# The opening of a streaming encoder layer: table load, row transfers, squares and rooms for modulation slabs rearranged

## The chip, the core and the metric

The kernel runs on one core of a Trainium2 chip. A core has a matrix engine (TensorE, PE in the profile), a vector engine (VectorE, DVE), a scalar engine (ScalarE, ACT), a general engine (GpSimd, POOL) and a synchronising engine (SyncE, SP). Each works off its own list of instructions in order. Transfers between memory and the core are issued here by SP and by ACT, as instructions in those lists. The metric is the device time of one execution in microseconds; the time before is the median of three runs.

## The reference

One layer of a hybrid encoder over 2048 prompt frames and 64 sample frames, 1024 channels each. A condition vector per stream gives six modulation vectors; the first two shift and scale the normalised input of the projection:

```python
mod = jax.nn.silu(c) @ p['w_ada'] + p['b_ada']
sh1, sc1, gt1, sh2, sc2, gt2 = [m[:, None, :] for m in jnp.split(mod, 6, axis=-1)]
h = rms_norm(x, p['norm1_g']) * (1 + sc1) + sh1
z = h @ p['w_in']
glu_a, glu_b, q, k, v, g_conv, g_attn = jnp.split(z, offs, axis=-1)
u = glu_a * jax.nn.sigmoid(glu_b)
conv_out, conv_state = conv_module(u, conv_hist, ...)      # depthwise width 31, layer norm, swish, projection
o = attend(rms_norm(q), rms_norm(k), v, p['rel_bias'])     # own chunk of 64 frames and the 8 before it
merged = sigmoid(g_conv) * conv_out + sigmoid(g_attn) * (o @ p['w_attn_out'])
x = x + gt1 * (merged @ p['w_o'])
# then a second modulated norm and a SwiGLU feed-forward of width 2816, with gt2
```

Everything is float32. The outputs are the two streams' rows, the last convolution rows, and the key and value rows.

## The kernel before

**Stages.** The 2112 rows are cut into four blocks (576, then three of 512). Each block goes through the projections q, k, v, the gated convolution inputs and the gates, while attention and convolution of earlier work run beside them. Then the merge, the output projection and the feed-forward run over three larger blocks of columns. Products of float32 are made of three matmuls each: weights and activations are split into a high part (ACT copies to the reduced format: `whi`, `hh`) and a low part (DVE or POOL subtracts: `wlo`, `hl`).

**The first block.** The change lies in what happens before and during the first projection, the function `first_block` and what it calls:

- `load_vectors` loads the two condition vectors (`r0`, two small transfers on ACT's queue), and later six small vectors (norm gains, convolution biases, `b_ada`) into `r1`, on SP's queue. `setup` turns `r0` into a column `cc` on PE, takes its tanh on ACT (the first function that needs ACT's table) and makes `cl` from it. Its inner function `vectors` turns `r1` into columns, `cols`.
- `Slabs` brings the modulation weights `w_ada` in slabs of 512 KB (`wmod`), into four rooms. For the first two vectors there are sixteen slabs; `modulation(ct)` uses four at a time, ct = 0, 2, 4, 6, and its part `rest` writes the columns `B1` and `A1` for two of the eight channel tiles. A slab's room is given back when PE has used it, and `fill` then issues the next load. The first four are shared between the queues of SP and ACT.
- `first_rows` loads the five row tiles of the block (64 rows, then four of 128), three on SP's queue and two on ACT's. `scale_rows` takes a row tile's sum of squares (`square`: two halves on ACT, one DVE addition, then a DVE operation and a power on POOL in `rsqrt_mean`) and scales the rows on DVE.
- `turn(k)` transposes channel tile k of all five row tiles on PE, applies `A1` and `B1` on DVE (`h32`), and splits into `hh` and `hl`. `product(i, k)` multiplies by the q weights, which `Weights` brings as `wst` tiles (512 KB each, at first one staging room, three after `W.open("wst")`) and splits.

**What sets the order.** Each engine's list is laid out when the kernel is built: an instruction's place follows the order in which the code makes it, as far as its inputs and its tile's room allow, by an estimate of times. `tc.issue_after(ins)` keeps instructions of the block, on the engine of `ins`, behind `ins`. Tiles with the same tag share a number of rooms (`bufs`); a tile that finds none waits for a release. Transfers of SP and ACT are counted on a small set of counters that go round in the order of issue. A host-side planner (`Stream`) keeps an estimated load per engine and spreads later work over PE's time; the tag `vv` (two rooms, first used by the relative bias rows `rv`, later by attention's v) and the tag `y` (one room, the convolution's output) belong to stages after the first projection.

Of the kernel before, what the change touches and what calls it, by code (L numbers as in the profile page):

```python
# [8 lines left out]
F32 = mybir.dt.float32  # L9
F32R = mybir.dt.float32r  # L10
AF = mybir.ActivationFunctionType
ALU = mybir.AluOpType
# [4 lines left out]
P = 128  # L17
D = 1024
KT = 8
# [210 lines left out]
class Slabs:  # L230
# [3 lines left out]
    def __init__(self, sync, other, pool, stream, keys, source, held):  # L234
        self.sync, self.other, self.pool, self.stream = sync, other, pool, stream
        self.keys, self.source, self.held = keys, source, held
        self.ready, self.used, self.given, self.freed = [], 0, 0, 0

    def fill(self):
        while len(self.ready) < min(len(self.keys), self.freed + self.held):  # L240
            (src,), a, b = self.source(self.keys[len(self.ready)])
            w = self.pool.tile([P, a, b], F32, tag="wmod", name="wmod", bufs=self.held)
            i = len(self.ready)
            (self.other if i < self.held and i % 2 else self.sync).dma_start(w, src)
            self.ready.append(w)

    def get(self, key):
        assert self.keys[self.used] == key
# [363 lines left out]
def streaming_layer(ctx: ExitStack, tc: tile.TileContext, I, O):  # L612
# [155 lines left out]
    def load_vectors():  # L768

        r0 = temp("r0", (16, P))  # L770
        r1 = temp("r1", (76, P))
        by_row = lambda a: a.rearrange("(r c) -> r c", c=P)
        nc.scalar.dma_start(r0[0:8], by_row(I["c_prompt"][0]))
        nc.scalar.dma_start(r0[8:16], by_row(I["c_sample"][0]))
        yield r0, r1
        o = 0
        for name in ("norm1_g", "norm2_g", "b_dw", "conv_ln_g", "conv_ln_b", "b_ada"):
            a = by_row(I[name][0])
            nc.sync.dma_start(r1[o : o + a.shape[0]], a)
            o += a.shape[0]  # L780
        yield

    def setup():
# [109 lines left out]

    def first_rows():
        places = ((wa, "x", 3), (wa, "x", 3), (wa, "x", 3), (wk, "kk", 1), (wk, "q2", 1))
        queues = (nc.sync, nc.sync, nc.scalar, nc.sync, nc.scalar)
        return [load_x(*tl, *place, q) for tl, place, q in zip(token_tiles(*PBLOCKS[0]), places, queues)]

    def first_block(xs):

# [1 line left out]
        vectors, taps, begun = setup()  # L902
        taps = taps()

        def scale_rows(a, b):
            for x_t, (t, n) in list(zip(xs, tiles))[a:b]:
                r = square(x_t, n)
                dve.tensor_scalar(x_t[:n], x_t[:n], r, None, ALU.mult)

        def modulation(ct):  # L910

# [27 lines left out]
        with tc.issue_after(begun[0]), tc.issue_after(begun[1]):  # L939
            scale_rows(0, 2)  # L940
            rest = modulation(0)
            vectors()
            rest()
            sums_turned = pe.last.ins
            with tc.issue_after(dve.last.ins):
                scale_rows(2, 5)
            with tc.issue_after(act.last.ins), tc.issue_after(dve.last.ins):
                W.reach = W.held
                W.fill()
        with tc.issue_after(sums_turned):  # L950
            turn(0)
        pss = [ps_g.tile([P, 512], F32, tag="gp", name="ps") for _ in tiles]
# [11 lines left out]
        for k in range(KT - 2):  # L964
            if k == 2:
                with tc.issue_after(act.last.ins):
                    next(taps)
            turn(k + 1)
            if k and k % 2 == 0:
                rest = modulation(k + 2)  # L970
            for i in range(len(tiles)):
                if i == 2 and not k:
                    rest = modulation(k + 2)
                    W.open("wst")
                if i == (2 if k else 4) and k % 2 == 0:
                    rest()
                product(i, k)
# [136 lines left out]
    def load_x(t, n, pool, tag, bufs, queue=nc.sync):  # L1114
        x_t = pool.tile([P, D], F32, tag=tag, name="x_t", bufs=bufs)
        queue.dma_start(x_t[:n], rows(x_p, x_s, t, n))
        return x_t

    def square(x_t, n):
# [1111 lines left out]
```

## Time and profile before

| | us |
|---|---|
| median of three runs | 3007.48 (3004.33 to 3010.57) |
| profiled execution | 3013.09 |
| its span, first to last instruction | 3011.3 |
| PE busy | 2927.7 |
| DVE busy | 2080.1 |
| ACT busy | 1291.3 |
| POOL busy | 1136.0 |

Rows of the timeline read: start, length, engine, line, operation, what it writes and from what, how many; in brackets the engine's idle time before it and what ended it. `ACTq` and `SPq` are the engines' own lists, where transfers are issued. All metered operations have line 102, that of the helper, so one goes by the names of tiles. Rows for a stretch read: stretch, length, then busy time and instructions of PE, weight loads, DVE, ACT and POOL, the granted PE clock, the share of the transfer engines, and GB/s. The chain of waits lists start, length and what the path stood on.

### The profile page before, as it was taken

How to read it: one execution, taken by the hardware profiler on the slowest of the kernel's cores; microseconds unless marked ns; L12 is line 12 of the kernel's file. 1: busy time of each engine (PE TensorE's matmuls, PEld its weight loads, DVE VectorE, ACT ScalarE, POOL GpSimd, SP SyncE). 2: the span in 40 equal slices, each digit the busy share in tenths (PEclk: the TensorE clock that was granted, in tenths of full speed). 3: DMA queues.
4: the chain of work that ended last, by engine and by line, in shares of the span. 5: the costliest groups of instructions: out<-in, count | busy, mean ns of one | idle time of the engine just before them, and what ended most of it. 6: DMA issues, size and time to landing. Idle time of an engine off the chain costs nothing.

```text
span 3011.3 us, 45036 instructions
## 1 busy us (share of the span) xinstructions
PE 2927.7 (97%) x16259; PEld 2599.9 (86%) x16259; DVE 2080.1 (69%) x3836; ACT 1291.3 (43%) x2333; POOL 1136.0 (38%) x734
## 2 busy tenths in 40 slices
PE   7999989999999999989999999999999999999999
PEld 4889767788888788888989899999999999999998
DVE  5888777877877886477776755666666556466666
ACT  3334532452254257464444435534444345344443
POOL 0201310101011102354566533256666841466667
PEclk9999899999999999999999999999999999999999
DMA  8888788888997788885444686423323875323333
GB/s 296 284 294 289 247 300 282 263 266 273 301 289 236 253 267 271 258 291 167 142 150 146 210 288 210 148 93 113 120 92 122 292 253 184 97 94 112 120 99 129
DMA packets 467725, 628.07 MB, mean 209 GB/s; under 512 B 36276, under 2 KB 314664, under 8 KB 467501
## 3 DMA queue, kind: packets, MB, share of 16 engines
q1 hardware_dynamic: 453456, 605.58, 61.6%
q10 hardware_dynamic: 14045, 19.60, 1.9%
q8 instruction: 128, 2.10, 0.3%
q14 instruction: 96, 0.79, 0.1%
HBM read 476.53 MB, written 148.54 MB: 208 GB/s over the span
## 4 chain that ended last, share of the span: by engine, by line
PE 79%; DVE 9%; DMA 6%; ACT 2%; issue 2%; POOL 2%; SPq 0%; ACTq 0%; POOLq 0%; DVEq 0%
PE ps L102 49%; PE pd L102 15%; PE pw L102 6%; DVE y L102 3%; PE po L102 2%; PE sc L102 2%; PE ptp L102 2%; DVE wlo L102 1%; PE pa L102 1%; PE pt L102 1%; DVE pr L102 1%; DMA wst<-in_w_in 1%; ACT whi L102 1%; POOL r L102 1%; POOL wlo L102 1%
## 5 line engine op out<-in xcount | busy, mean ns | idle before, releaser
L102 PE MATMUL ps<-t,whi 128*128 128x384 f32 (+1 forms) x2112 | 502.8, 322 | 9.6 <-ACT t L102 4.6
L102 POOL TENSOR_TENSOR wlo<-wst,whi 128x1024 fp32r<-128x1024 f32 (+1 forms) x157 | 357.9, 2290 | 272.2 <-ACT whi L102 258.2
L102 ACT ACTIVATE whi<-wst 128x1024 fp32r<-128x1024 f32 (+1 forms) x264 | 257.5, 978 | 331.8 <-PE ps L102 105.0
L102 PE MATMUL ps<-b,whi 128*128 128x384 f32 (+1 forms) x1584 | 381.7, 326 | 6.0 <-DVE early L102 3.4
L102 PEld LDWEIGHTS ps<-t,whi 128*128 128x128 f32 x2112 | 367.7, 188 | 16.9 <-ACT t L102 4.8
L102 DVE SCALAR_TENSOR_TENSOR y<-u,wd,y 128x512 f32<-128x512 f32 (+1 forms) x480 | 370.2, 773 | 5.8
L102 PE MATMUL ps<-hh,whi 128*128 128x512 f32 (+2 forms) x992 | 363.7, 367 | 0.0
L102 DVE TENSOR_TENSOR acc<-acc,pd 128x512 f32<-128x512 f32 (+1 forms) x464 | 311.6, 685 | 66.8 <-PE pd L102 64.4
L102 PE MATMUL ps<-hh,wlo 128*128 128x512 f32 (+2 forms) x992 | 347.7, 350 | 0.0
L102 PE MATMUL ps<-hl,whi 128*128 128x512 f32 (+2 forms) x992 | 347.0, 350 | 0.0
L102 PE MATMUL ps<-t,wlo 128*128 128x384 f32 (+1 forms) x1056 | 339.3, 321 | 0.7 <-POOL wlo L102 0.7
L102 PE MATMUL pd<-whi,hid 128*128 128x512 f32 (+1 forms) x1016 | 325.5, 391 | 0.2 <-DVE acc L102 0.2
L102 PEld LDWEIGHTS ps<-b,whi 128*128 128x128 f32 x1584 | 278.8, 190 | 12.1 <-DVE early L102 4.2
L102 PE MATMUL ps<-b,wlo 128*128 128x384 f32 (+1 forms) x792 | 257.0, 325 | 0.0
L102 POOL TENSOR_TENSOR r<-t,mhalf 128x1 f32<-128x1 f32 (+3 forms) x68 | 81.7, 1203 | 456.5 <-DVE t L102 449.6
L102 PEld LDWEIGHTS pd<-whi,hid 128*128 128x128 f32 (+1 forms) x1016 | 185.9, 183 | 45.5 <-DVE acc L102 1.1
L102 PEld LDWEIGHTS ps<-hh,wlo 128*128 128x128 f32 x992 | 188.2, 190 | 22.2
L102 PEld LDWEIGHTS ps<-hh,whi 128*128 128x128 f32 x992 | 188.7, 190 | 18.2 <-issue 2.5
L102 PEld LDWEIGHTS ps<-hl,whi 128*128 128x128 f32 x992 | 189.0, 191 | 15.6 <-issue 1.7
L102 PEld LDWEIGHTS ps<-t,wlo 128*128 128x128 f32 x1056 | 198.2, 188 | 2.2 <-POOL wlo L102 1.3
L102 PE MATMUL pd<-wlo,hid 128*128 128x512 f32 (+1 forms) x508 | 198.5, 391 | 0.0
L102 DVE TENSOR_TENSOR wlo<-wst,whi 128x1024 fp32r<-128x1024 f32 (+1 forms) x107 | 133.7, 1255 | 82.1 <-ACT whi L102 80.6
(225 smaller groups left out, 6255.1 us busy)
## 6 DMA issues: line engine op xcount, KB each, us to landing
whi<-w_din_h SPq DMA_DIRECT2D x72, 512.0 KB, 7.0
wlo<-w_din_l SPq DMA_DIRECT2D x72, 512.0 KB, 7.3
wst<-sum_d SPq DMA_DIRECT2D x132, 256.0 KB, 2.8
wfo<-in_w_ffn_out SPq DMA_DIRECT2D x64, 512.0 KB, 3.4
wmod<-in_w_ada SPq DMA_DIRECT2D x46, 512.0 KB, 7.5
sum_d<-ws SPq DMA_DIRECT2D x88, 256.0 KB, 3.1
wst<-in_w_ffn_in SPq DMA_DIRECT2D x84, 256.0 KB, 3.1
wst<-in_w_in SPq DMA_DIRECT2D x40, 512.0 KB, 8.0
```

The lines of the kernel that those rows point to most:

```text
L102: self.last = f(*args, **kw)
```

## The change

Five edits, all for the first block:

- The six small vectors of `r1` are loaded on ACT's queue, behind the tanh, instead of on SP's queue ahead of the rows. `vectors` now runs after the first sums of the modulation.
- All five row tiles are loaded on SP's queue.
- The square of a first-block row is one ACT operation over 1024 elements, written to a part of `hl` that isn't used yet, with no addition behind it. The fifth row is scaled on ACT, after the first weight's split, instead of on DVE; the third row's scaling is placed ahead of `rest`.
- Slabs 4 to 7 go to four lent rooms (two of tag `vv`, two halves of the convolution's `y`), so that they can be loaded before the first four rooms are free, and slabs 8 to 11 follow into the first four rooms.
- The staging rooms for weights are opened at once; the first split alone is made early, and the others where the rooms were opened before.

```diff
@@ class Slabs
+    def room(self):
+        i = len(self.ready)
+        if self.lent is None:
+            return i < self.held
+        n = len(self.lent)
+        return i < self.freed + self.held + (n if i < self.held + n + self.held else 0)

     def fill(self):
-        while len(self.ready) < min(len(self.keys), self.freed + self.held):
+        while len(self.ready) < len(self.keys) and self.room():
             (src,), a, b = self.source(self.keys[len(self.ready)])
-            w = self.pool.tile([P, a, b], F32, tag="wmod", name="wmod", bufs=self.held)
             i = len(self.ready)
+            if i >= self.held and i - self.held < len(self.lent):
+                w = self.lent[i - self.held]().rearrange("p (a b) -> p a b", a=a)
+            else:
+                w = self.pool.tile([P, a, b], F32, tag="wmod", name="wmod", bufs=self.held)
...
+    def lend(self, rooms):
+        self.lent = rooms
+        self.fill()
@@ load_vectors
-            nc.sync.dma_start(r1[o : o + a.shape[0]], a)
+            nc.scalar.dma_start(r1[o : o + a.shape[0]], a)
@@ setup
         act_th = act.last.ins
+        with tc.issue_after(act_th):
+            next(vectors_)
@@ first_rows
-        queues = (nc.sync, nc.sync, nc.scalar, nc.sync, nc.scalar)
-        return [load_x(*tl, *place, q) for tl, place, q in zip(token_tiles(*PBLOCKS[0]), places, queues)]
+        return [load_x(*tl, *place) for tl, place in zip(token_tiles(*PBLOCKS[0]), places)]
+
+    def lent_rooms():
+        conv_room = wk.tile([P, 4, YW], F32, tag="y", name="ym").rearrange("p c w -> p (c w)")
+        v_room = lambda: wk.tile([P, D], F32, tag="vv", name="vm", bufs=2)
+        return [v_room, v_room, lambda: conv_room[:, :D], lambda: conv_room[:, D : 2 * D]]
@@ first_block
+        def square_row(i):
+            return square(xs[i], tiles[i][1], hl[:, KT - 2 :, :512])
...
             rest = modulation(0)
-            vectors()
-            rest()
+            with tc.issue_after(pe.last.ins), tc.issue_after(dve.last.ins):
+                vectors()
+                scale_rows(2, 3)
+            with tc.issue_after(dve.last.ins):
+                rest()
             sums_turned = pe.last.ins
             with tc.issue_after(dve.last.ins):
-                scale_rows(2, 5)
+                scale_rows(3, 4)
+                r = square_row(4)
             with tc.issue_after(act.last.ins), tc.issue_after(dve.last.ins):
-                W.reach = W.held
+                W.reach = 1
                 W.fill()
+            with tc.issue_after(act.last.ins):
+                act.activation(xs[4], xs[4], AF.Copy, scale=r)
...
                     rest = modulation(k + 2)
-                    W.open("wst")
+                    W.reach = W.held
+                    W.fill()
@@ square
+        if room is not None:
+            act.activation(room[:n], x_t[:n].rearrange("p (a b) -> p a b", a=2), AF.Square, accum_out=ssq[:n, 0:1])
+            stream.after("dve", "act")
+            return rsqrt_mean(wk, ssq[:n, 0:1], n, 1, D)
@@ main
     M.fill()
-    next(vectors_)
     xs = first_rows()
     W = Weights(...)
+    M.lend(lent_rooms())
+    W.open("wst")
     first_block(xs)
```

More of the change, by code (lines that the diff above doesn't have):

```diff
@@ L237, in __init__ @@
         self.ready, self.used, self.given, self.freed = [], 0, 0, 0
+        self.lent = None
+    def room(self):
[4 more added lines that the diff above has]
+        return i < self.freed + self.held + (n if i < self.held + n + self.held else 0)
     def fill(self):
-        while len(self.ready) < min(len(self.keys), self.freed + self.held):
+        while len(self.ready) < len(self.keys) and self.room():
             (src,), a, b = self.source(self.keys[len(self.ready)])
-            w = self.pool.tile([P, a, b], F32, tag="wmod", name="wmod", bufs=self.held)
             i = len(self.ready)
+            if i >= self.held and i - self.held < len(self.lent):
+                w = self.lent[i - self.held]().rearrange("p (a b) -> p a b", a=a)
+            else:
+                w = self.pool.tile([P, a, b], F32, tag="wmod", name="wmod", bufs=self.held)
             (self.other if i < self.held and i % 2 else self.sync).dma_start(w, src)
             self.ready.append(w)
+    def lend(self, rooms):
+        self.lent = rooms
+        self.fill()
     def get(self, key):
@@ L903, in first_block @@
         taps = taps()
+        def square_row(i):
+            return square(xs[i], tiles[i][1], hl[:, KT - 2 :, :512])
         def scale_rows(a, b):
-            for x_t, (t, n) in list(zip(xs, tiles))[a:b]:
-                r = square(x_t, n)
-                dve.tensor_scalar(x_t[:n], x_t[:n], r, None, ALU.mult)
+            for i in range(a, b):
+                n, r = tiles[i][1], square_row(i)
+                dve.tensor_scalar(xs[i][:n], xs[i][:n], r, None, ALU.mult)
         def modulation(ct):
@@ L1117, in load_x, with square @@
         return x_t
-    def square(x_t, n):
+    def square(x_t, n, room=None):
         ssq = wk.tile([P, 2], F32, tag="ssq", name="ssq", bufs=3)
+        if room is not None:
+            act.activation(room[:n], x_t[:n].rearrange("p (a b) -> p a b", a=2), AF.Square, accum_out=ssq[:n, 0:1])
+            stream.after("dve", "act")
+            return rsqrt_mean(wk, ssq[:n, 0:1], n, 1, D)
         for j in range(2):
```

## The prediction

> **What bounds the kernel now.** I read the page first, then stretches of equal length, then the chain of waits at the start. The page says that TensorE (PE) is the bound over the whole run; the stretches say where it is not.
>
> ```profile
> span 3011.3 us, 45036 instructions
> PE 2927.7 (97%) x16259; PEld 2599.9 (86%) x16259; DVE 2080.1 (69%) x3836; ACT 1291.3 (43%) x2333; POOL 1136.0 (38%) x734
> ```
>
> ```profile
> 0.00:50.00 50.00, 29.32 (x186) 18.58 (x187) 22.99 (x66) 15.31 (x32) 4.27 (x14) 1.00 0.86 270
> 50.00:100.00 50.00, 48.86 (x302) 38.20 (x301) 34.39 (x63) 18.13 (x29) 9.14 (x9) 1.00 0.88 305
> 400.00:450.00 50.00, 41.95 (x185) 30.51 (x183) 35.19 (x82) 14.93 (x36) 6.97 (x6) 0.88 0.90 291
> ```
>
> PE idles 83.6 us in all (3011.3 less 2927.7), and 20.7 us of that lies in the first 50. The change touches the start alone, so it can win some of these 20.7 us and no more. The start as it runs now, by the chain of waits and then the timeline:
>
> ```profile
> 0.73 2.66 DMA r<-in_c_prompt
> 3.41 7.56 DMA x_t<-in_x_prompt
> 10.99 0.35 ACTq L1116
> 11.37 1.28 ACT L102
> 13.35 3.69 PE pa L102 x32
> ```
>
> ```profile
> 1.70 0.97 ACTq L244 DMA_DIRECT2D wmod<-in_w_ada  x2
> 1.78 0.80 SPq L779 DMA_DIRECT2D r<-in_norm_g  x2
> 4.91 0.25 SPq L779 DMA_DIRECT2D r<-in_b_dw  x1
> 5.55 0.17 DVE L102 COPY cc<-pt 128x16 f32<-128x16 f32 x1 [3.60 <-PE pt L102]
> 8.31 0.32 SPq L779 DMA_DIRECT2D r<-in_b_ada  x1
> 9.51 0.30 ACTq L989 DMA_DIRECT2D rv<-in_rel_bias  x1
> 11.67 0.36 PE L102 MATMUL pt<-ident,r 76*128 76x76 f32 x1 [6.15 <-DMA r<-in_b_ada]
> 12.66 0.21 ACT L102 ACTIVATE th<-cc 128x16 f32<-128x16 f32 x1
> 12.79 0.61 ACT L102 ACTIVATE junk<-x_t 64x512 f32<-64x512 f32 x1
> 18.21 0.63 ACT L102 ACTIVATE junk<-x_t 128x512 f32<-128x512 f32 x1 [2.80 <-issue]
> 21.29 0.61 ACT L102 ACTIVATE junk<-x_t 128x512 f32<-128x512 f32 x1
> 21.90 1.04 ACT L102 ACTIVATE whi<-wst 128x1024 fp32r<-128x1024 f32 x1
> 24.61 0.75 DVE L102 TENSOR_SCALAR x_t<-x_t,r 128x1024 f32<-128x1024 f32 x1 [0.66 <-POOL r L102]
> 28.84 0.78 PE L102 MATMUL ps<-whi,hh 128*64 128x512 f32 x1
> ```
>
> To be seen: the column `cc` is ready at 5.72, but its tanh runs at 12.66. ACT was standing in its own queue: the row tile issued at 3.41 landed at 10.97, and only then (10.99) did the next issue go, and the table load at 11.37. So an issue can wait for the landing of an earlier transfer that has nothing to do with it. SP shows the same: after 2.58 its next tiny load goes at 4.91. The first product stands at 28.84, 3.48 us after the fifth row tile was scaled (24.61 + 0.75 = 25.36).
>
> **The change part by part.** *Rows on SP, table loaded early.* ACT is free of transfers at 2.67 (1.70 + 0.97). The table load of 1.28 then ends at about 4, and tanh follows `cc` at 5.75: 6.9 us earlier. The sums of the first four slabs (3.69 us) then wait for the slabs. Four slabs are 2.10 MB, the five row tiles 2.36 MB, the first weight 0.52 MB.
>
> ```profile
> 2.00:17.00 15.00, 4.26 (x34) 1.75 (x34) 2.06 (x11) 4.03 (x10) 1.07 (x4) 1.00 1.00 332
> 60.00:70.00 10.00, 10.00 (x52) 7.62 (x51) 3.94 (x12) 1.75 (x2) 0.00 (x0) 1.00 1.03 402
> 26.00:34.00 8.00, 6.19 (x44) 3.73 (x45) 6.76 (x13) 4.30 (x6) 0.00 (x0) 1.00 0.28 76
> 90.00:110.00 20.00, 20.00 (x97) 15.46 (x96) 18.03 (x24) 4.30 (x7) 0.21 (x1) 1.00 1.02 340
> ```
>
> At 332 GB/s from 2.0 us the four slabs are there by 8.3, the rows by 9.1, 10.7, 12.3, 13.8 and 15.4, the first weight by 17.0, the four lent slabs by 23.3. The sums so end near 10, not at 17.04. They are no longer what is late; the rows are. The Trainium skill (DMA: Bandwidth & Descriptors, Specifications) puts the HBM share of a core at about 358 GB/s; by that, as an estimate, the fifth row would land 0.9 us earlier, at 14.5. The trace doesn't bear it out as a limit (402 GB/s from 60 to 70); the sum goes by the measured 332.
>
> *Six small loads moved from SP to ACT, behind tanh, ahead of the squares.* This is the unknown of the change. Each takes 0.25 to 0.40 us of issue (rows at 1.78 to 8.31), and each may wait for the landing of an earlier transfer, as ACT did at 10.99. Lower bound: no wait, six issues end at 5.95 + 6 x 0.3 = 7.8, and the squares wait only for rows. Upper bound: all of SP's new queue was issued before them, and the last of the six waits for the fourth lent slab, 23.3. I take 12.5: between the issue of the slabs and that of the six, SP has some four or five row tiles out, so the last waits are for row tiles, of which the third lands at 12.3. The vectors are then at PE 3.36 us after the last issue (11.67 less 8.31), by 15.9. What follows them:
>
> ```profile
> 19.57 1.22 PE L102 MATMUL pa<-sel,R 128*128 128x128 f32 x4 [0.54 <-DVE B L102]
> 20.83 0.16 DVE L102 TENSOR_TENSOR A<-pa,cols 128x4 f32<-128x4 f32 x1 [1.32 <-PE pa L102]
> ```
>
> Some six small DVE operations at 0.16 to 0.23 take them to 17.0; the edit puts the third row's scaling (0.75) ahead of the rest, 17.8; one more of 0.16, the second four matmuls (1.22) and two of 0.16 end at 19.5. The rows are later, as the next two steps show.
>
> *Squares in one operation.* Two halves start 0.61 to 0.63 apart. One operation over 1024 I price by the weight split of that size, 1.04, and 0.02 between: 1.06 for 1.24, and the DVE addition (0.15) behind it goes. Five rows from 12.5 end at 17.8. Rows four and five have landed (13.8, 15.4). No gap of 2.80 stands between second and third any more.
>
> *Fifth row scaled on ACT.* After the square come the weight split (1.05; the weight is there at 17.0) and the scaling, priced like the split, 1.05: done at 19.9. POOL's power for that row fits under the split. Hence the first product follows the start of the squares by 5.3 + 2.1 + 3.4 = 10.8: 12.5 + 10.8 = 23.3. **Term 1: 28.84 to 23.3, -5.5** (bounds: squares limited by the fifth row alone, first product 22.5, -6.3; upper bound 23.3 + 10.8 = 34.1, +5.3).
>
> *Second slabs in lent rooms, weights opened early.* The transfer engines are busy 0.28 of the time from 26 to 34 now: 5.8 us lost while slabs wait for rooms. With four more rooms, slabs and two weights go on without the gap. What PE waits for later in this pass:
>
> ```profile
> 47.59 0.71 PE L102 MATMUL pa<-sel,R 128*128 128x128 f32 x4 [1.70 <-DVE R L102]
> 57.06 0.64 PE L102 MATMUL pa<-wmod,cl 128*32 128x256 f32 x8 [0.41 <-DMA wmod<-in_w_ada]
> 58.43 0.64 PE L102 MATMUL pa<-wmod,cl 128*32 128x256 f32 x8 [0.73 <-DMA wmod<-in_w_ada]
> ```
>
> ```profile
> 35.69 8.91 DMA wst<-in_w_in
> ```
>
> ```profile
> ACT whi L102 <- DMA wmod<-in_w_ada: 3.8, 1, 3.8
> ```
>
> The wait of 1.70 stands behind a weight that landed at 44.60; by bytes it now lands by 36 (11.3 MB up to it at 332 GB/s). **Term 2: -1.7.** The 0.41 and 0.73 are for the last slabs, which still come one for one; I leave them (bound: -1.1 more). *The load of the bias table* (`rv`, 9.51 now) loses its early room to a slab and is issued on ACT in the middle of the pass, where ACT already stood 3.8 us behind an issue that waited for a slab. Bounds 0 and +3.8; I take 0, since PE did not stop at that wait (its only waits there are the three above).
>
> *What is kept.* -5.5 and -1.7 make -7.2 at the end of the pass. From 90 to 110 the transfers are full (1.02), so what is bound by bytes there can move up only by the idle 5.8 us filled. I take the middle of 5.8 and 7.2: **-6.5**. The later gaps move with the rest. The profiled execution took 3013.09 us, 5.6 above the median of the three runs, 3007.48; it would give 3006.6, and the median 3001.0.
>
> **The rivals.** *ACT stands behind its own small loads* (ends slower). For: the rows at 3.41 and 10.99 show the mechanism, and the six loads now stand ahead of all squares on the same engine. Against: tanh comes early, when SP can have issued little. With the squares starting at s, the first product is at s + 10.8; s = 19.7 eats both terms. At the upper bound, 34.1, it is +5.3 - 1.7 = +3.6, and with the bias load's 3.8 hitting the products +7.4: 3014.9. It passes +6 when s is over 21.9 and ACT stands 3.8 us again in the pass. In its mild form (s of 15 to 20) the time is 3004 to 3008.
>
> *The gain is swallowed.* The stretch at 90 to 110 is full of transfers and 0.90 of DVE; if DVE's work there doesn't move up, the PE gap behind it grows by what was won: 3007.5. Against: DVE's input is PE's output, which comes earlier.
>
> *A later gap opens.* In 400 to 450 PE lost 8.05 us (50 less 41.95) at a granted clock of 0.88; a shifted order could bring one more such gap: -6.5 + 8.05, 3009.0. Nothing in the rows says that it must. The Trainium skill (TensorE: Matmul & The Clock Gate, HAM oscillation) says that PE gaps beyond about 3.4 us bring the half clock back; the 0.88 of that row agrees with the rule, and it would make such a gap dearer than its idle time.
>
> *All bounds at their good end*: -6.3 - 1.7 - 1.1 = -9.1: 2998.4.
>
> **How the numbers follow.** Forecast 0.53 (-9 to -3: 2998.5 to 3004.5); small loads, mild 0.10, hard 0.15; swallowed 0.09; later gap 0.08; all good 0.05. About 0.2%, 6.0 us, is what a measurement here can tell from none. The forecast lies on that edge: 0.33 of its chance beyond it, 0.20 within. Faster 0.33 + 0.05 = 0.38; within 0.20 + 0.10 + 0.09 + 0.08 = 0.47; slower 0.15. The range, 2997.5 to 3013.5, takes in the good end and all but the worst of the small loads; the forecast's own is 2998.5 to 3004.5.
>
> **What would show it.** Tanh before 7; the first sums at PE ending near 10; squares starting near 12.5, as one operation of about 1.06 each; the fifth row scaled on ACT near 20; the first product at 22 to 25; no stretch of idle transfers between 26 and 34; no wait of 1.7 for R; the end of the pass 6 to 8 us before 75. Wrong it would be if the squares start after 16, if ACT's small loads show issue times spread over ten microseconds, or if the pass ends early and the stretch from 100 on doesn't.

## The result, and the profile after

The changed kernel takes 3014.45 us (median of 17 runs, 3007.10 to 3015.63), the kernel before, run beside it, 3010.13 us (17 runs, 3001.97 to 3014.52). The ratio is 1.0015, with a 95% interval of 1.0008 to 1.0022: slower by about 4.5 us, where 6.5 us less was forecast, and outside the range given. The two profiled executions (3013.09 before, 3012.72 after) lie at different places of their kernels' spreads, so their spans don't show the difference. The stages of the start do. Everything below is read from those.

The head of the page after:

```profile
span 3010.9 us, 45020 instructions
```

The timeline of the start after (start, length, engine, line, operation, tiles, count, and in brackets the idle time before it with what ended it):

```profile
2.37 9.56 SPq L1149 DMA_DIRECT2D x_t<-in_x_prompt  x4
2.69 1.28 ACT L102 ACT_TABLE_LOAD   x1 [2.69 <-issue]
5.28 0.21 ACT L102 ACTIVATE th<-cc 128x16 f32<-128x16 f32 x1 [1.30 <-DVE cc L102]
5.28 1.09 ACTq L795 DMA_DIRECT2D r<-in_norm_g  x2
5.97 1.08 PE L102 MATMUL pa<-wmod,cl 128*32 128x256 f32 x8 [0.94 <-DVE cl L102]
11.63 1.93 PE L102 MATMUL pa<-wmod,cl 128*32 128x256 f32 x16 [4.58 <-DMA wmod<-in_w_ada]
15.41 0.25 ACTq L795 DMA_DIRECT2D r<-in_b_dw  x1
15.43 1.08 PE L102 MATMUL pa<-wmod,cl 128*32 128x256 f32 x8 [1.87 <-DMA wmod<-in_w_ada]
16.46 0.32 ACTq L795 DMA_DIRECT2D r<-in_b_ada  x1
16.83 1.06 ACT L102 ACTIVATE hl<-x_t 64x1024 fp32r<-64x1024 f32 x1 [11.34 <-DMA r<-in_conv_ln_b]
...
21.55 1.06 ACT L102 ACTIVATE hl<-x_t 128x1024 fp32r<-128x1024 f32 x1
...
25.20 0.16 DVE L102 TENSOR_TENSOR A<-A,cols 128x4 f32<-128x4 f32 x1
25.28 0.15 DVE L102 TENSOR_SCALAR t<-ssq 128x1 f32<-128x1 f32 x1
26.77 0.15 DVE L102 TENSOR_SCALAR t<-ssq 128x1 f32<-128x1 f32 x1
26.83 1.21 DVE L102 TENSOR_TENSOR wlo<-wst,whi 128x1024 fp32r<-128x1024 f32 x1
26.99 1.46 POOL L102 TENSOR_TENSOR r<-t,mhalf 128x1 f32<-128x1 f32 x1 [0.93 <-DVE t L102]
28.49 1.15 ACT L102 ACTIVATE x_t<-x_t,r 128x1024 f32<-128x1024 f32 x1 [4.83 <-POOL r L102]
32.63 0.77 PE L102 MATMUL ps<-whi,hh 128*64 128x512 f32 x1
```

To be seen, from the top:

- The table load is early and tanh runs at 5.28 instead of 12.66. The first eight sums start at 5.97 (before: 13.35).
- But PE then stops for a slab until 11.63, and for the last slab until 15.43. The sums end at 16.51, where they ended at 17.04 before. Nearly the whole early start is lost to slabs that come late.
- ACT issues the first two of its six small loads at 5.28 and the third at 15.41. That is 0.02 us before PE picks up the last slab: the issue waited for that slab's landing, just as PE did (the same pair stands in the run with the fourth and fifth row ahead of the columns: 14.88 and 14.90). Its other loads follow in a row, and the squares start at 16.83 (before: 12.79).
- The squares themselves are one operation of 1.06, and all five are through at 22.61. The fifth row is scaled on ACT, but only at 28.49: ACT waited 4.83 us for the row's factor `r`. The DVE operation that feeds it (`t`, at 26.77) stands behind the modulation columns (`A`, 25.20) and the fourth row in DVE's list.
- The first product is at 32.63, 3.79 us later than before (28.84).

Why the slabs come late is told by the packets of the two queues (q1 is SP's, q10 ACT's: packets, MB, share of the 16 transfer engines). From 9 to 11 us after:

```profile
q1 hardware_dynamic: 152, 0.56, 77.1%
q10 hardware_dynamic: 154, 0.15, 23.3%
```

and from 7 to 9 us before:

```profile
q10 hardware_dynamic: 531, 0.74, 109.2%
q1 hardware_dynamic: 8, 0.00, 0.5%
```

After, the two queues have the same number of packets in that stretch, 152 and 154. But a packet of the rows is 3.7 KB (0.56 MB by 152), one of the slabs 1.0 KB. So SP's rows take 79% of the bytes, and the two slabs on ACT's queue get 75 GB/s. From 7 to 13 us together it is 409 and 424 packets, 1.48 and 0.42 MB. Before, SP had no row out until 8.68 (one row stood on ACT's own queue, behind its slabs), and between 7 and 9 us ACT's queue moved 0.74 MB, 370 GB/s, alone. The Trainium skill (DMA: Bandwidth & Descriptors, Queues, rings and completion order) says that a transfer engine goes round the queues that have work and takes a packet from each before it goes on. The trace agrees from 7 to 13 us: packets are shared evenly, and bytes by the size of the packets.

The later part of the pass. The end of the first pass is read at the first transposition of `r` that follows it. Before:

```profile
75.43 0.25 PE L102 MATMUL pt<-ident,r 31*128 31x31 f32 x1
```

After:

```profile
52.28 0.33 ACTq L836 DMA_DIRECT2D cc<-in_cache_conv  x1
53.04 1.06 ACT L102 ACTIVATE whi<-wst 128x1024 fp32r<-128x1024 f32 x1 [7.37 <-DMA wmod<-in_w_ada]
54.72 0.44 PE L102 MATMUL ps<-whi,hh 128*64 128x512 f32 x1 [1.89 <-ACT hh L102]
79.00 0.24 PE L102 MATMUL pt<-ident,r 31*128 31x31 f32 x1
```

The waits of 1.70, 0.41 and 0.73 are gone. In their place PE waits 1.89 for `hh`, which ACT makes at 54.00, just behind a weight split that waited 7.37 us behind two small loads at 52.28 and 52.65. From the first product to this row the kernel takes 46.37 us (79.00 less 32.63), before 46.59. So the 3.79 us lost at the first product are 3.57 at the end of the pass, and about 4.5 in the time. The stretches (stretch, length, busy time of PE, weight loads, DVE, ACT and POOL, granted clock, share of the transfer engines, GB/s). The pass before:

```profile
28.84:75.43 46.59, 43.75 (x272) 29.85 (x270) 27.66 (x53) 13.93 (x20) 1.20 (x1) 1.00 0.89 298
```

Three stretches after:

```profile
26.00:34.00 8.00, 3.35 (x10) 2.23 (x11) 5.01 (x11) 3.82 (x5) 1.52 (x2) 1.00 1.06 351
32.63:79.00 46.37, 44.48 (x273) 31.22 (x271) 27.66 (x53) 13.81 (x20) 1.20 (x1) 0.96 0.76 261
55.00:59.00 4.00, 4.00 (x12) 3.03 (x11) 2.94 (x6) 0.68 (x1) 0.00 (x0) 0.57 0.99 283
```

The hole in the transfers between 26 and 34 is filled (1.06, before 0.28). It is merely moved: over the pass their share falls from 0.89 to 0.76. And the pass holds a loss that isn't a wait: behind the wait of 1.89 PE's granted clock falls to half (0.57 from 55 to 59, 0.50 from 56 to 58), and a product that takes 0.40 us around it takes 0.63. Eight of them start some 0.42 us apart instead of 0.23, which is about 1.5 us. PE's idle time in the pass falls from 2.84 to 1.89, but its busy time grows from 43.75 to 44.48 (the rest of the 1.5 is made up elsewhere in the pass). Before, the granted clock was 1.00 through the whole pass.

### The profile page after: what moved, and what is told of

It reads as the page before. It is cut to its first block, busy times and chain, and to the rows that moved or that the text cites. A ratio compares the mean times of both kernels' runs of the same rounds, so it can differ in the third digit from the quotient of the medians.

```text
span 3010.9 us, 45020 instructions
## 1 busy us (share of the span) xinstructions
PE 2925.1 (97%) x16259; PEld 2596.9 (86%) x16259; DVE 2079.6 (69%) x3830; ACT 1291.5 (43%) x2324; POOL 1137.2 (38%) x734
## 4 chain that ended last, share of the span: by engine, by line
PE 77%; DVE 9%; DMA 7%; ACT 2%; issue 2%; POOL 2%; SPq 1%; ACTq 0%; DVEq 0%; POOLq 0%
PE ps L102 49%; PE pd L102 16%; PE pw L102 6%; DVE y L102 3%; PE po L102 2%; PE sc L102 2%; PE ptp L102 2%; DVE wlo L102 1%; DVE pr L102 1%; PE pt L102 1%; PE pa L102 1%; ACT whi L102 1%; DMA kk<-k_d 1%; DMA wmod<-in_w_ada 1%; POOL r L102 1%
```

## The experiments

The theory: slabs and rows share the transfer engines packet by packet, so rows that go out early hold the slabs back; ACT's small loads, placed behind tanh, wait for a slab and hold the squares; and the fifth row is held again by DVE's order. The rivals: ACT's own loads are the whole loss, with the slabs late for another reason; DVE's order alone is; the lent rooms cost time; rows on one queue are bad by themselves. Each of the first runs takes away one of these. "First product" and "end of the pass" are the two rows named above; before they are 28.84 and 75.43, after 32.63 and 79.00. Ratios are to the kernel before, with a 95% interval.

### The small loads back on SP, ahead of the rows

```diff
@@ load_vectors
-            nc.scalar.dma_start(r1[o : o + a.shape[0]], a)
+            nc.sync.dma_start(r1[o : o + a.shape[0]], a)
@@ setup
-        with tc.issue_after(act_th):
-            next(vectors_)
@@ main
     M.fill()
+    next(vectors_)
     xs = first_rows()
```

> The changed kernel with the six small vectors back on SP's queue, ahead of the rows; all else as changed. Theory S (rows issued from 1.8 us take the transfer engines from the first four slabs, the fourth of which landed at 15.4): with the six small loads ahead, the rows go out after 8 us again, the fourth slab lands by 10, the sums end by 11 instead of 16.5, squares start near 13 as the rows land; first product 25 to 27 instead of 32.6; the time 4 to 7 us below the changed kernel. Theory Q (only ACT's own queue was the loss): squares start as soon as the first row lands, but the sums still end near 16; first product 28 to 30.

Measured: 3009.52 us, ratio 1.0003 (0.9991 to 1.0015); first product 27.55, end of the pass 74.96. The timeline:

```profile
7.65 2.45 PE L102 MATMUL pa<-wmod,cl 128*32 128x256 f32 x24 [0.70 <-DMA wmod<-in_w_ada]
7.99 0.58 SPq L1147 DMA_DIRECT2D x_t<-in_x_sample  x1
11.49 1.06 ACT L102 ACTIVATE hl<-x_t 64x1024 fp32r<-64x1024 f32 x1 [6.09 <-DMA x_t<-in_x_sample]
23.40 1.15 ACT L102 ACTIVATE x_t<-x_t,r 128x1024 f32<-128x1024 f32 x1 [2.64 <-POOL r L102]
```

The small loads now hold SP, so the rows go out at 7.99 instead of 1.77. The slabs have the engines to themselves, and the sums end at 10.1, as forecast for the change itself. The squares start at 11.49. What the small loads did on SP in the kernel before is plain here: they kept the rows back until the slabs were in. The first product is 5.1 us earlier than after, yet 16.06 behind the squares' start, not 10.8: the wait for `r` is still there (2.64), and the squares now wait for rows between them, 2.2 us in all.

### The small loads issued by GpSimd

```diff
@@ load_vectors
-            nc.scalar.dma_start(r1[o : o + a.shape[0]], a)
+            nc.gpsimd.dma_start(r1[o : o + a.shape[0]], a)
@@ setup
-        with tc.issue_after(act_th):
-            next(vectors_)
@@ main
     M.fill()
+    next(vectors_)
```

> The changed kernel with the six small vectors issued by GpSimd, so that neither SP nor ACT issues them, and the rows still go out from 1.8 us. Theory S: the fourth slab still lands at 14 to 16 and the sums end near 16; squares are free and start when the rows land (10 to 13), first product 27 to 30. Theory Q: with ACT free the whole loss is gone, first product 23 to 25.

Measured: 3009.16 us, ratio 1.0001 (0.9992 to 1.0011); first product 29.55, end of the pass 76.58. The timeline:

```profile
1.78 0.57 SPq L1147 DMA_DIRECT2D x_t<-in_x_sample  x1
10.10 1.06 ACT L102 ACTIVATE hl<-x_t 64x1024 fp32r<-64x1024 f32 x1 [4.62 <-DMA x_t<-in_x_sample]
11.52 1.93 PE L102 MATMUL pa<-wmod,cl 128*32 128x256 f32 x16 [4.49 <-DMA wmod<-in_w_ada]
17.14 1.08 PE L102 MATMUL pa<-wmod,cl 128*32 128x256 f32 x8 [3.69 <-DMA wmod<-in_w_ada]
```

ACT is free here, and the squares start when the first row lands, at 10.10. The fourth slab still comes at 17.14, after the fifth row. So the late slabs are not ACT's doing: with the rows out at 1.78 on the other queue they are late whatever ACT does. Both halves of the theory are needed: the rows crowd out the slabs (this run), and ACT's loads carry that delay over to the squares (6.7 us between this run's 10.10 and 16.83).

### All four first slabs on SP's queue

```diff
@@ class Slabs, fill
-            (self.other if i < self.held and i % 2 else self.sync).dma_start(w, src)
+            self.sync.dma_start(w, src)
```

> The changed kernel with all four first slabs on SP's queue, ahead of the rows, and nothing else changed. Theory S1 (two queues share the engines unevenly: rows of 4 KB runs on SP's queue crowd out the slabs of 1 KB runs on ACT's, while inside one queue the order of issue holds): the fourth slab lands by 10 and the sums end by 11, though the rows still follow at once. Theory S2 (all transfers in flight share alike, whatever the queue): the fourth slab still lands at 14 to 16. By S1 the small loads' issues end by 14 and the first product is at 28 to 30; by S2 it stays at 32 to 33.

Measured: 3010.95 us, ratio 1.0007 (0.9996 to 1.0017); first product 30.05, end of the pass 75.60. The timeline:

```profile
6.40 2.80 PE L102 MATMUL pa<-wmod,cl 128*32 128x256 f32 x24 [0.94 <-DVE cl L102]
10.80 0.64 PE L102 MATMUL pa<-wmod,cl 128*32 128x256 f32 x8 [1.61 <-DMA wmod<-in_w_ada]
13.28 0.33 ACTq L795 DMA_DIRECT2D r<-in_b_ada  x1
13.65 1.06 ACT L102 ACTIVATE hl<-x_t 64x1024 fp32r<-64x1024 f32 x1 [7.73 <-DMA r<-in_conv_ln_g]
```

The rows are out early here too, but behind the slabs in the same queue. The fourth slab is there at 10.80 instead of 15.43, and the last small load goes out 3.2 us earlier. On one queue the order of issue does hold; across two it does not. That is what the first step of the prediction left out.

### The kernel before, with its rows on one queue

```diff
@@ first_rows (kernel before)
-        queues = (nc.sync, nc.sync, nc.scalar, nc.sync, nc.scalar)
-        return [load_x(*tl, *place, q) for tl, place, q in zip(token_tiles(*PBLOCKS[0]), places, queues)]
+        return [load_x(*tl, *place) for tl, place in zip(token_tiles(*PBLOCKS[0]), places)]
```

> The kernel before with one part of the change alone: all five rows on SP's queue, behind the six small loads. ACT is then not held by the row issued at 3.4. If the early table load is worth something by itself, tanh runs near 5.5 instead of 12.7, the sums end near 10 instead of 17.0, and the first product is at 26 to 28 instead of 28.8, the time 1 to 3 us below before. If the rows were the limit all along, the first product is at 28 to 30.

Measured: 3010.56 us, ratio 1.0009 (0.9998 to 1.0019); first product 28.76, end of the pass 79.05. Tanh runs at 5.50 here, and the sums end at 14.2, 2.9 us earlier than before, as the third and fifth row no longer hold ACT. The first product doesn't move (28.76 against 28.84). The columns `A` are ready 0.9 us earlier (20.10), but behind them DVE takes the last three rows one at a time, 1.67 us apart, and scales the last at 24.54 (before 24.61), though its square was there at 20.34. An early tanh by itself is worth nothing as long as DVE's list behind the columns ends the start. The pass behind it is 3.7 us longer than before: PE waits 4.54 in it instead of 2.84, and the clock falls to half there too (0.50 from 61 to 63).

### The changed kernel, with the third and fifth row back on ACT's queue

```diff
@@ first_rows
-        return [load_x(*tl, *place) for tl, place in zip(token_tiles(*PBLOCKS[0]), places)]
+        queues = (nc.sync, nc.sync, nc.scalar, nc.sync, nc.scalar)
+        return [load_x(*tl, *place, q) for tl, place, q in zip(token_tiles(*PBLOCKS[0]), places, queues)]
```

> The changed kernel with the third and fifth row tiles back on ACT's queue, all else as changed. The small loads then stand behind two rows and two slabs on ACT, and behind tanh. If each issue waits for the landing of the eighth transfer before it, ACT's issue of a row waits for the first slab, tanh comes later than 5.3, the squares start at 17 to 19 and the first product is at 32 to 35: no better than the changed kernel. If rows on one queue were the cause of the crowding, the fourth slab lands by 11 and the first product is at 28 to 30.

Measured: 3008.24 us, ratio 0.9996 (0.9986 to 1.0005); first product 35.19, end of the pass 79.02. The timeline:

```profile
13.80 1.08 PE L102 MATMUL pa<-wmod,cl 128*32 128x256 f32 x8 [0.69 <-DMA wmod<-in_w_ada]
17.77 0.32 ACTq L795 DMA_DIRECT2D r<-in_b_ada  x1
18.14 1.06 ACT L102 ACTIVATE hl<-x_t 64x1024 fp32r<-64x1024 f32 x1 [11.44 <-DMA wst<-in_w_in]
```

With fewer row bytes on SP's side the fourth slab is 1.6 us earlier (13.80 against 15.43). ACT's queue now has two rows behind that slab, and the small loads wait for those: the squares start later still. The first product is 2.6 us later than after, and the end of the pass the same to 0.02. In between, ACT's wait ahead of a split at the mid-pass small loads is 1.97 instead of 7.37, and PE's wait of 1.89 for `hh` is gone; one of 0.69 for a slab is left. That is 1.2 of the 2.6. The other 1.3 is PE's busy time, 43.14 us in this pass instead of 44.48: its clock stays at 1.00. The time is even lower than after's: the end of the pass and the time don't go together to better than some 5 us. That is taken up below.

### The fourth and fifth row ahead of the columns in DVE's list

```diff
@@ first_block
                 vectors()
-                scale_rows(2, 3)
+                scale_rows(2, 4)
+                r = square_row(4)
             with tc.issue_after(dve.last.ins):
                 rest()
             sums_turned = pe.last.ins
-            with tc.issue_after(dve.last.ins):
-                scale_rows(3, 4)
-                r = square_row(4)
```

> The changed kernel with the fourth row's scaling and the fifth row's square placed ahead of the modulation columns on DVE. Theory O (DVE's order holds the fifth row: ACT waited 4.83 us for its power): the fifth row is scaled by 25 instead of 29.6, the first product at 29 to 30 instead of 32.6, the time 2 to 4 us below the changed kernel. If order is not a cause, first product stays at 32 to 33.

Measured: 3010.12 us, ratio 1.0000 (0.9989 to 1.0011); first product 30.09, end of the pass 74.93. The timeline:

```profile
16.30 1.06 ACT L102 ACTIVATE hl<-x_t 64x1024 fp32r<-64x1024 f32 x1 [10.74 <-DMA r<-in_conv_ln_b]
25.53 1.15 ACT L102 ACTIVATE x_t<-x_t,r 128x1024 f32<-128x1024 f32 x1 [2.40 <-POOL r L102]
```

The late slabs and the late squares (16.30) are left as they are. The wait for `r` falls from 4.83 to 2.40, and the first product follows the squares' start by 13.79 instead of 15.80. The first product is 2.5 us earlier (0.5 of it from squares that started earlier in this execution), the end of the pass about 4 (PE idles 0.81 in this pass, and its clock stays at 1.00), and the changed kernel is back at the level of the one before.

### Both: small loads on SP, rows ahead of the columns

The edit is that of the first experiment (small loads on SP) and of the one just above (rows ahead of the columns) together.

> The changed kernel with both mends together: small vectors on SP ahead of the rows, and the fourth and fifth rows ahead of the modulation columns on DVE. If both causes (crowded slabs, DVE's order) are real and add, the fifth row is scaled by 22.5, the first product is at 25 to 26 (27.6 with the first mend alone), the end of the pass near 73, the time 2 to 4 us below before. If the order is no cause once the rows come late, the first product stays at 27 to 28 and the time equals before.

Measured: 3004.77 us, ratio 0.9989 (0.9980 to 0.9999): faster than the kernel before, though the interval only just leaves out 1. First product 25.06, end of the pass 73.14. The timeline:

```profile
7.77 2.79 PE L102 MATMUL pa<-wmod,cl 128*32 128x256 f32 x24 [0.49 <-DMA wmod<-in_w_ada]
11.91 1.06 ACT L102 ACTIVATE hl<-x_t 64x1024 fp32r<-64x1024 f32 x1 [6.20 <-DMA x_t<-in_x_sample]
20.50 1.15 ACT L102 ACTIVATE x_t<-x_t,r 128x1024 f32<-128x1024 f32 x1 [0.32 <-POOL r L102]
25.06 0.77 PE L102 MATMUL ps<-whi,hh 128*64 128x512 f32 x1
```

The squares' start (11.91) is now near the 12.5 of the prediction, the fifth row's scaling (20.50) near its 19 to 20, and the first product 1.8 us behind its 23.3, since the last rows land one by one. Both faults repaired, the other edits do win: 3.8 us at the first product, 2.3 at the end of the pass, 3.3 in the time. It is still half of what was forecast. Of the 1.5 lost on the way from 3.8 to 2.3, 0.64 are waits of PE and 0.85 its busy time, with the clock at half again (0.52 from 55 to 58).

### Slabs on SP, small loads on ACT ahead of the table load, rows ahead of the columns

```diff
@@ class Slabs, fill
-            (self.other if i < self.held and i % 2 else self.sync).dma_start(w, src)
+            self.sync.dma_start(w, src)
@@ setup
-        with tc.issue_after(act_th):
-            next(vectors_)
@@ main
     first_vectors = next(vectors_)
+    next(vectors_)
     M = Slabs(...)
```

and `first_block` as in the experiment on DVE's list.

> The changed kernel with all four first slabs on SP's queue ahead of the rows, the six small vectors on ACT directly behind the condition vectors (ahead of the table load), and the fourth and fifth rows ahead of the modulation columns on DVE. Theory S1: slabs by 10, rows by 16, squares as the rows land, first product at 23 to 25, the end of the pass near 71, the time 4 to 6 us below before. Theory S2: sums end at 14 to 16 and the first product is at 27 or later; the time equals before.

Measured: 3006.84 us, ratio 0.9995 (0.9983 to 1.0007); first product 27.16, end of the pass 73.72. The small loads, on ACT ahead of its table load, put the table load to 5.45 and tanh to 6.74; the squares start at 13.35, when the rows land. The first product was expected at 23 to 25 and missed that by two, with the slabs and rows landing later than reckoned (PE takes up the fourth slab at 12.05). That ACT may issue the small loads without harm if they go ahead of everything else is so: they are all issued by 5.42, as nothing large stands before them on that queue.

### The lent rooms: without, with, and used twice

Without the rooms, first in the changed kernel:

```diff
@@ class Slabs
-        if self.lent is None:
-            return i < self.held
-        n = len(self.lent)
-        return i < self.freed + self.held + (n if i < self.held + n + self.held else 0)
+        return i < self.freed + self.held
...
-            if i >= self.held and i - self.held < len(self.lent):
-                w = self.lent[i - self.held]().rearrange("p (a b) -> p a b", a=a)
-            else:
-                w = self.pool.tile([P, a, b], F32, tag="wmod", name="wmod", bufs=self.held)
+            w = self.pool.tile([P, a, b], F32, tag="wmod", name="wmod", bufs=self.held)
@@ first_block
-                    W.fill()
+                    W.open("wst")
@@ main
-    M.lend(lent_rooms())
-    W.open("wst")
```

> The changed kernel without the lent rooms, with weights opened where they were before. If the early slabs and weights add to the crowding at the start, first product is earlier than 32.6 by 1 to 2 us; if they are neutral there, it is 32 to 33. In the pass, the wait of 1.70 for R and the idle transfer engines after the first slabs come back, and the end of the pass is 1 to 2 us later than the changed kernel's 79.0, if the rooms win what was forecast for them; the same 79.0 if they win nothing.

Measured: 3017.64 us, ratio 1.0029 (1.0018 to 1.0040), the slowest of all; first product 34.93, end of the pass 81.13. Its stretch and the wait that the rooms were to take away:

```profile
26.00:34.00 8.00, 3.18 (x10) 1.88 (x10) 3.59 (x10) 1.68 (x3) 2.01 (x2) 1.00 0.35 107
```

The transfers have their hole again (0.35), and PE waits 1.68 for `R` at 53.84, as before. The rooms do what the prediction's fifth step says, then. They are not the cause of the loss: it is larger without them. But at the end of the pass none of the extra is theirs: from the first product to it the kernel takes 46.20 here and 46.37 with the rooms. The 2.1 us are lost ahead of the first product: the bias table's load goes out early again on ACT, ahead of the table load, the second small load of ACT then ends at 16.48 (6.37 with the rooms), and the squares start at 18.08.

The same edit on the kernel with both faults repaired:

> The kernel with both mends, without the lent rooms and with the weights opened where they were before. Without lent rooms the wait for R behind a late weight (1.70 in the kernel before) and idle transfer engines near 26 to 34 come back: end of the pass at 75 to 76 instead of 73.1, the time equal to before or 1 us below. If the rooms are worth nothing in the mended kernel, the end stays at 73.

Measured: 3006.50 us, ratio 0.9991 (0.9982 to 1.0000); first product 26.23, end of the pass 73.69, where 75 to 76 was expected. The rooms are worth 1.2 us at the first product and 0.55 at the end of the pass there; the two times, 3004.77 and 3006.50, can't be told apart by their intervals. PE's waits in the pass are 0.87, 0.98, 1.75 and 0.82 without the rooms and 0.55, 0.99 and 1.95 with them, 0.9 us less. That gain is lost to the clock in these two executions: without the rooms it stays at 1.00 in the pass and PE is busy 43.04 us, with them it is 0.94 and PE is busy 44.60.

The rooms used a second time, for slabs 12 to 15, on the kernel with both faults repaired:

```diff
@@ class Slabs
-        return i < self.freed + self.held + (n if i < self.held + n + self.held else 0)
+        return i < self.freed + self.held + (n if i < 2 * (self.held + n) else 0)
...
-            if i >= self.held and i - self.held < len(self.lent):
-                w = self.lent[i - self.held]().rearrange("p (a b) -> p a b", a=a)
+            n = len(self.lent or ())
+            if i < 2 * (self.held + n) and i % (self.held + n) >= self.held:
+                w = self.lent[i % (self.held + n) - self.held]().rearrange("p (a b) -> p a b", a=a)
```

> The kernel with both mends (small vectors on SP, rows ahead of the columns), and the four lent rooms given to slabs 12 to 15 as well. In the mended kernel PE still waited 0.99 and 1.95 for the last slabs in the first pass. If those waits are for want of rooms, they go, and the end of the pass comes at 70 to 71 instead of 73.1, the time 2 to 3 us below the mended kernel's. If the transfer engines are the limit there, other waits (for weights, for ACT) take their place and the end stays at 73.

Measured: 3004.93 us, ratio 0.9982 (0.9973 to 0.9991), faster than both kernels; first product 25.37, end of the pass 74.86, where 70 to 71 was expected. The timeline of PE:

```profile
47.55 0.84 PE L102 MATMUL pt<-ident,x_t 64*128 64x64 f32 x5 [2.96 <-DVE h L102]
49.63 0.69 PE L102 MATMUL ps<-whi,hh 128*64 128x512 f32 x1 [1.24 <-ACT hh L102]
```

No wait for a slab is left in the pass. DVE's `h` and ACT's `hh` are late in its place, 4.20 us in the two rows, against 3.49 in the three waits of the kernel with the rooms lent once. The other half of the lost time is the clock, 0.50 from 50 to 54: PE is busy 45.29 us in this pass, against 44.60 with the rooms lent once. So bytes aren't the bound of this stretch once they come early.

### What stays open

The start is accounted for; how it turns into time, only roughly. Part of the scatter is the half clock in the first pass:

| kernel | pass, first product to end | PE idle in it | PE busy in it | granted clock |
|---|---|---|---|---|
| before | 46.59 | 2.84 | 43.75 | 1.00 |
| before, rows on one queue | 50.29 | 4.54 | 45.75 | 0.97 |
| after | 46.37 | 1.89 | 44.48 | 0.96 |
| after, two rows back on ACT's queue | 43.83 | 0.69 | 43.14 | 1.00 |
| both faults repaired | 48.08 | 3.48 | 44.60 | 0.94 |
| the same, no lent rooms | 47.46 | 4.42 | 43.04 | 1.00 |
| the same, rooms used twice | 49.49 | 4.20 | 45.29 | 0.91 |

What brings the half clock on is not shown. Behind the wait of 1.89 it came, behind one of 1.70 before and one of 1.75 without the rooms it didn't. Nor is it known whether it falls at the same place in every execution, as one of each kernel was traced. Differences of a microsecond or so at the end of the pass are therefore not the edit's alone. Over the whole run the clock doesn't seem to be what makes the changed kernel slower: its mean over the 17 runs is 0.9925, and 0.991 in the runs of the kernel before beside the experiments.

At the same end of the pass, 79.0, three kernels have ratios of 1.0015, 1.0009 and 0.9996. At 73 to 75 they lie between 0.9982 and 1.0003. The direction holds (81.1 has 1.0029), the sizes scatter by 0.1 to 0.2%. Later in the run the same work falls into another order, and no run here was aimed at that.

## Why the prediction was wrong, point by point

- *Rows on SP, table early.* Right: ACT is free, the table load ends at 3.97, tanh runs before 7 (5.28). **Wrong, and the first step that failed: "the four slabs are there by 8.3", "the sums so end near 10, not at 17.04".** The total rate was right (333 GB/s from 2 to 17, the forecast's 332). The order wasn't: I let bytes land in order of issue over both queues. The last slab came at 15.41 and the sums ended at 16.51. The run with all slabs on SP's queue shows the order of issue holding within one queue, and the one with GpSimd's small loads that the slabs are held back by early rows with ACT free of loads, too.
- *Six small loads on ACT.* The mechanism and its bounds (7.8 to 23.3) were right, the value of 12.5 was 4.3 too low: 16.83. It assumed that the last waits are for row tiles; the third load waited for the fourth slab. Given the slab's true landing, the step would have given 16.8 at once.
- *Squares in one operation.* Right: 1.06 each. But they come 1.18 apart, where the step reckoned 1.06 from one to the next; 0.5 us over five rows.
- *Fifth row on ACT.* **The second step that failed: "the first product follows the start of the squares by 5.3 + 2.1 + 3.4 = 10.8".** Measured: 15.80, made of 5.78 for the squares, 1.04 for the split, a wait of 4.83, the scaling of 1.15 and 2.99 to the product. Nearly the whole miss is the wait. "POOL's power for that row fits under the split" looked at POOL alone; the operation that feeds it stands on DVE behind `B`, `A` and the fourth row. With that order mended the wait is 2.40, and with the slabs in time too, 0.32. Term 1 became +3.8 instead of -5.5: 4.3 from the squares' start and 5.0 from this step.
- *Lent rooms.* Right in what they do: no idle transfers from 26 to 34, no wait of 1.70 for `R`. The term of -1.7 was -0.2. The three waits of 2.84 us in all went, but one of 1.89 took their place, behind the 7.37 us in which ACT stood ahead of its mid-pass small loads; and behind that wait the clock fell to half, so that PE's busy time in the pass grew by 0.73. The bias table's load itself held nothing up (it went out at 35.98). The wait that mattered is the one of 3.8 from which I took its upper bound, and which I priced at 0 "since PE did not stop at that wait". It was twice as long, and then PE did.
- *What is kept.* Nothing was won, so this step had nothing to carry. The loss was kept: 3.57 at the end of the pass, about 4.5 in the time.
- *The rivals.* What happened is the rival "ACT stands behind its own small loads", with its mechanism and both its signs (squares after 16, issues spread over ten microseconds: 5.28 to 16.46). Its price was worked out by the same 10.8, so for squares that start between 15 and 20 it gave 3004 to 3008, not slower; it was to end clearly slower only from 21.9 on. With 15.8 in that place the first product is late as soon as the squares start after 13.0 (28.84 less 15.8). Of the 13.45 us between forecast and result, 2.65 come from the kernel before, whose median over 17 runs is 3010.13 and not 3007.48; the sign was wrong without them. *A later gap* reckoned with the half clock behind gaps beyond about 3.4 us. In the row that it read, 400 to 450, PE's two longest gaps were 3.13 and 3.39, each with the half clock near it; in the changed kernel's pass it came behind a gap of 1.89. So a rule by the length of one gap doesn't fit these traces.

## What to carry to other kernels

When transfers go out on two queues, don't add up bytes in order of issue: here the queues took turns by packets, the one with the larger packets got most of the bytes (79%), and what is needed first belongs ahead in the same queue, or alone in time. A row of small loads that looks like overhead can be what holds a large transfer back at the right moment; before moving it, look at what starts when it is gone. And for every operation that is moved to another engine, follow the list of the engine that makes its last input: a value that seems to come from a free engine may stand third in a busy one. When a pass is longer or shorter by a microsecond, look at the granted clock in it as well as at the waits.

## What the runs showed of the hardware that was not expected

- *Queues share by packets.* From 9 to 11 us the packets were 152 and 154, the bytes 0.56 and 0.15 MB (shown above). The same holds in the run with GpSimd's small loads, 132 and 138 packets, 0.50 and 0.14 MB. It doesn't hold from the first: from 3 to 5 us after, SP's queue moved 733 packets and ACT's 16, though ACT's two slabs were issued by 2.66. Why was not tried, and no run changed the size of the packets.
- *An issue waits for an old transfer.* ACT's third small load and SP's last row went out just as PE picked up a slab: the small load at 15.41 beside 15.43, the row at 11.6 (the four issues of 2.37 end at 11.93) beside 11.63. The small load has nothing to do with the slab; ACT stood 9.0 us for it (5.28 + 1.09 to 15.41).
- *The clock falls to half inside a pass.* After, it was 0.50 from 56 to 58 us, and the same product took 0.63 instead of 0.40 us. It did so in the middle of the pass in six of the changed or partly changed kernels and not in the kernel before. The first products of the pass take 0.63 as well, in both kernels (at 30.27 before, at 34.06 after), while the clock reads 1.00 there; so the reading doesn't show every slow stretch.
- *The read of a square's sum is on the path now.* Behind each square stands a read of the accumulator, 0.18 to 0.19 us. In the kernel before the next half started ahead of its end (read at 18.75, next half at 18.84); now the next square starts behind it. The halves wrote to rooms that take turns, the squares all write to the same part of `hl`; that this is the reason was not tried.

```profile
17.80 0.18 ACT L102 ACTIVATION_READ_ACCUMULATOR hl<-x_t 64x1 f32 x1
18.01 1.06 ACT L102 ACTIVATE hl<-x_t 128x1024 fp32r<-128x1024 f32 x1
```

- *POOL's small power is slowed by DVE.* On 128 x 1 elements it takes 0.55 to 0.57 us, but 1.46 in the changed kernel, where DVE's subtraction `wlo` of two tensors (26.83, 1.21 us) runs beside it (26.99). For the fifth row it is 1.46 in five of the kernels, the changed one among them, each time with `wlo` beside it, and 0.55 in the kernel before, in the one with its rows on one queue, and in the five with the fourth and fifth row ahead of the columns, where `wlo` comes later; in the run with GpSimd's small loads two powers beside and behind `wlo` take 2.34 together. The Trainium skill (GPSIMD Engine Reference, Specifications) says that GpSimd shares its SBUF interfaces with VectorE and that the two contend when DVE works on two inputs from SBUF; the trace agrees, with 0.9 us for one tiny operation on the path.
